# Output projections as seven half-size products, with weight sums made in DRAM

## The chip, the cores and the metric

The kernel runs on one core of a Trainium2 chip. The metric is device time in microseconds (us); lower is better. The engines are TensorE (PE: matmuls into PSUM, with PEld for the load of the stationary side), VectorE (DVE), ScalarE (ACT), GpSimd (POOL) and SyncE (SP, which issues most DMAs). Three runs of the kernel before took 1337.84, 1338.29 and 1338.46 us.

## The reference

The reference is a trunk of two layers on 512 tokens of width 2048, all in float32. Each layer is one mixer with two groups of heads, and an RMS norm closes the trunk:

```python
for l in range(DEPTH):                       # 2
    h = rmsnorm(x, attn_norm_g[l])
    qa, ka, va, ga, cq, ckv, kr, gb = jnp.split(h @ w_in[l], SPLIT_POINTS, axis=-1)
    ya = swa_attention(qa, ka, va, swa_sinks[l]) * jax.nn.silu(ga)      # 16 heads of 64, window 128
    yb = mla_attention(cq, ckv, kr, ...) * jax.nn.silu(gb)              # 8 latent heads of 128, causal
    x = x + jnp.concatenate([ya, yb], axis=-1) @ w_out[l]               # 512x2048 @ 2048x2048
return rmsnorm(x, final_norm_g)
```

The change concerns the line with `w_out`, the residual beside it and the last norm.

## The kernel before

**Products in three parts.** Every operand is split into a part `hi`, rounded by a cast on ACT, and the rest `lo`, a subtraction on DVE; `split` does both. A product is three matmuls, hi x hi, hi x lo and lo x hi (`mm3`, lines 115 to 118).

**The stream.** All dense products (input projection, gates, output projection) are one list, `stream`, of pieces. A `Piece` is four row blocks of 128 of one column tile of 128: it loads 512 KB for two pieces on SP's queue into one of three raw buffers (`RBUF`), splits a 128x512 part, and then gives four steps of three matmuls, 128x128 weights against 512 tokens. Weights are the stationary side; the result has features on partitions and tokens along the free axis. `prefetch` issues loads and splits `AHEAD` (3) items ahead of their use. `fill(n)` takes n steps from the stream; the attention code calls it between its own parts, with the counts in `FILLS`, so that PE has dense work while ACT and DVE do the softmax.

**Heads.** Each of eight turns does two sliding-window heads and one latent head: scores (`swa_scores`, `mla_scores`), softmax, transposes of the probabilities on PE (`swa_transpose`, `mla_transpose`; their results are split on DVE and ACT), products with the values, and the gate (`gated`, line 827), which gives `y`, a block of 128 features x 512 tokens. `put_y` keeps it, and it is split when the output projection begins.

**Output projection.** For each of 16 column tiles, 16 row blocks x 3 matmuls add up in one PSUM bank. `out_fin` (layer 0) adds the residual, which `load_res` fetched by DMA, squares the sum on ACT, adds the square into `acc` on POOL (`square_into`, line 176), stores x to DRAM and splits it for layer 1. `token_sums` (line 152) later turns `acc` into sums per token by matmuls with ones. The first layer's x is squared in the same way while it is loaded. In layer 1, `last_fin` does the adding and squaring, and the last three column tiles are computed for 256 tokens at a time, so that `finish` can scale and store the first half while the second is computed.

**What sets the order.** The program is written for a framework that orders each engine's instructions itself, by the program's order as priority and by what it reckons to be ready; tiles from a pool wait until a buffer is free. At run time each engine executes its list in order, and waits where an operand is not there.

## Time and profile before

| | |
|---|---|
| median of three runs | 1338.29 us |
| span of the profiled execution | 1336.3 us |
| PE, DVE, ACT, POOL busy | 99%, 65%, 48%, 6% |
| output projection of layer 0 | about 516 to 690 us |
| output projection of layer 1, with the end | about 1163 to 1336 us |
| DMA traffic | 131.73 MB, 99 GB/s on average |

The profiled execution's own time is known by its span; the runs' median lies 2.0 us above it. Busy times of PE overlap (a matmul starts before the one before it has drained), so work on PE is counted by the distance from one start to the next. DVE's overlap a little too. A wait names the instruction that released the waiting one.

### The profile page before, as it was taken

Reading aid. Unit: us, or ns where it says so; the run is one execution under the profiler, and the core shown is the slowest. Engines: PE = TensorE matmul, PEld = TensorE weight load, DVE = VectorE, ACT = ScalarE, POOL = GpSimd, SP = SyncE. Lnnn points to the kernel's source line nnn. Section 1 sums busy time; section 2 is a strip of 40 time slices with the busy share of each in tenths; the row PEclk is TensorE's granted clock in tenths of the full one; section 3 lists DMA queues with packets and bytes.
Section 4 is the critical chain, followed back from the end, with each engine's and each line's share of the span. In section 5 each row is a group of like instructions: output and inputs, shape, how many; then the busy total and the mean of one; then the engine's idle time right before and its main releaser. Section 6 shows DMA issues by size and latency. Waiting matters only on the chain.

```text
span 1336.3 us, 18300 instructions
## 1 busy us (share of the span) xinstructions
PE 1320.6 (99%) x6534; PEld 1114.7 (83%) x6534; DVE 867.2 (65%) x2067; ACT 637.0 (48%) x1373; POOL 78.2 (6%) x77
## 2 busy tenths in 40 slices
PE   9999999999999999999999999999999999999996
PEld 6888888888888888888888888888888888888896
DVE  5578877777777786444434787776876878733344
ACT  5546545555544564333323454554554555543331
POOL 4310000000000000111101000000000000011112
PEclk9999999999999999999999999999999999999998
DMA  6532221222221224444333313213213222233333
GB/s 205 173 122 69 80 86 59 79 89 72 79 81 64 72 68 145 147 146 149 116 88 113 120 54 107 79 49 96 80 54 105 65 65 84 88 114 126 123 103 126
DMA packets 49739, 131.73 MB, mean 99 GB/s; under 512 B 5584, under 2 KB 12800, under 8 KB 49648
## 3 DMA queue, kind: packets, MB, share of 16 engines
q1 hardware_dynamic: 49136, 129.54, 30.5%
q8 instruction: 51, 0.84, 0.3%
q0 software_dynamic: 512, 1.03, 0.2%
q14 instruction: 40, 0.33, 0.1%
HBM read 122.15 MB, written 8.39 MB: 98 GB/s over the span
## 4 chain that ended last, share of the span: by engine, by line
PE 96%; DVE 2%; ACT 1%; DMA 1%; issue 0%; SPq 0%; DVEq 0%; ACTq 0%
PE ps L116 29%; PE ps L117 29%; PE ps L118 29%; PE ps L661 2%; PE ps L806 1%; PE ps L637 1%; PE ps L597 1%; PE ps L596 1%; PE ps L781 1%; PE ps L780 1%; PE ps L287 1%; PE ps L286 1%; PE ps L152 0%; DMA blk<-in_xT 0%; PE ps L167 0%; DMA wraw<-in_w_lr 0%
## 5 line engine op out<-in xcount | busy, mean ns | idle before, releaser
L116 PE MATMUL ps<-blk,whi 128*128 128x512 f32 x1456 | 573.7, 394 | 0.3 <-ACT blk L112 0.3
L117 PE MATMUL ps<-blk,whi 128*128 128x512 f32 x1456 | 568.0, 390 | 0.3 <-DVE blk L113 0.3
L118 PE MATMUL ps<-blk,wlo 128*128 128x512 f32 x1456 | 567.7, 390 | 0.0
L108 ACT CAST whi<-wraw 128x512 fp32r<-128x512 f32 x356 | 221.0, 621 | 406.7 <-PE ps L117 380.0
L109 DVE TENSOR_TENSOR wlo<-wraw,whi 128x512 fp32r<-128x512 f32 x356 | 248.3, 699 | 187.8 <-ACT whi L108 183.3
L118 PEld LDWEIGHTS ps<-blk,wlo 128*128 128x128 f32 x1456 | 273.3, 188 | 58.1 <-DVE wlo L109 0.2
L116 PEld LDWEIGHTS ps<-blk,whi 128*128 128x128 f32 x1456 | 273.8, 188 | 54.1 <-ACT blk L112 0.7
L117 PEld LDWEIGHTS ps<-blk,whi 128*128 128x128 f32 x1456 | 273.9, 188 | 53.9 <-DVE blk L113 0.9
L176 POOL TENSOR_TENSOR blk<-blk 128x512 f32<-128x512 f32 (+1 forms) x52 | 65.9, 1268 | 1240.8 <-ACT blk L175 1240.6
L116 PE MATMUL ps<-blk 128*128 128x256 f32 (+3 forms) x376 | 123.9, 329 | 0.6 <-ACT blk L108 0.6
L117 PE MATMUL ps<-blk 128*128 128x256 f32 (+3 forms) x376 | 122.5, 326 | 0.0
L118 PE MATMUL ps<-blk 128*128 128x256 f32 (+3 forms) x376 | 122.5, 326 | 0.0
L108 ACT CAST blk<-blk 128x512 fp32r<-128x512 f32 (+2 forms) x146 | 81.5, 576 | 48.5 <-DVE blk L644 21.0
L109 DVE TENSOR_TENSOR blk<-blk 128x512 fp32r<-128x512 f32 (+2 forms) x146 | 90.9, 636 | 13.7 <-ACT blk L108 7.0
L116 PEld LDWEIGHTS ps<-blk 128*128 128x128 f32 x376 | 71.3, 190 | 8.0 <-ACT blk L108 2.2
L109 DVE TENSOR_TENSOR blk<-ps,blk 128x512 fp32r<-128x512 f32 (+2 forms) x116 | 64.9, 585 | 19.4 <-ACT blk L108 16.5
L117 PEld LDWEIGHTS ps<-blk 128*128 128x128 f32 x376 | 71.3, 190 | 6.3 <-DVE blk L109 0.4
L118 PEld LDWEIGHTS ps<-blk 128*128 128x128 f32 x376 | 71.2, 189 | 5.7 <-DVE blk L109 0.4
L616 ACT ACTIVATE blk<-blk,sm 128x256 f32<-128x256 f32 (+1 forms) x128 | 60.1, 471 | 23.9 <-DVE sm L614 22.9
L108 ACT CAST blk<-ps 128x512 fp32r<-128x512 f32 (+2 forms) x116 | 54.7, 509 | 34.2 <-PE ps L118 22.2
L113 DVE SCALAR_TENSOR_TENSOR blk<-blk,g_in_sb 128x512 fp32r<-128x512 f32 x32 | 34.1, 1066 | 26.3 <-ACT blk L112 26.2
L604 DVE CUSTOM_DVE_ANT_0 blk<-ps,dist_sb,sdiv_sb 128x256 f32<-128x256 f32 x96 | 43.3, 479 | 0.8 <-PE ps L597 0.8
(156 smaller groups left out, 1137.9 us busy)
## 6 DMA issues: line engine op xcount, KB each, us to landing
wraw<-in_w_in SPq DMA_DIRECT2D x104, 512.0 KB, 3.5
wraw<-in_w_out SPq DMA_DIRECT2D x58, 512.0 KB, 3.5
wraw<-in_w_lr SPq DMA_DIRECT2D x32, 352.0 KB, 3.0
blk<-in_xT SPq DMA_DIRECT2D x32, 256.0 KB, 3.7
blk<-in_w_kv SPq DMA_DIRECT2D x16, 256.0 KB, 4.2
x_scr<-blk SPq DMA_DIRECT2D x16, 256.0 KB, 2.1
blk<-x_scr SPq DMA_DIRECT2D x16, 256.0 KB, 3.8
out_x<-blk SPq DMA_DIRECT2D x16, 256.0 KB, 2.6
```

The costliest lines, as they stand in the source:

```text
L108: nc.scalar.copy(hi, src)
L109: nc.vector.tensor_tensor(out=lo, in0=src, in1=hi.bitcast(F32), op=ALU.subtract)
L113: nc.vector.scalar_tensor_tensor(out=lo, in0=src, scalar=g, in1=hi.bitcast(F32), op0=ALU.mult, op1=ALU.subtract)
L116: nc.tensor.matmul(ps, lhsT=lh, rhs=rh, start=first, stop=False)
L117: nc.tensor.matmul(ps, lhsT=lh, rhs=rl, start=False, stop=False)
L118: nc.tensor.matmul(ps, lhsT=ll, rhs=rh, start=False, stop=last)
L176: nc.gpsimd.tensor_tensor(out=acc, in0=acc, in1=sq, op=ALU.add)
L286: nc.tensor.matmul(ps[5], lhsT=hb[:, P:2 * P], rhs=ah, start=kt == 0, stop=False)
L287: nc.tensor.matmul(ps[5], lhsT=hb[:, P:2 * P], rhs=al, start=False, stop=kt == KT - 1)
L604: nc.vector.tensor_tensor_reduce(out=pt, in0=o, in1=bias, scale=1.0, scalar=sdiv_sb[:, l, h:h + 1], op0=ALU.add, op1=ALU.max, accum_out=mx ...
L616: nc.scalar.activation(pv[qb], pv[qb], AF.Exp, bias=nb[:, qb:qb + 1], scale=SLOPES[h], accum_out=sm[:, qb:qb + 1])
L661: nc.tensor.matmul(av[:, w], lhsT=st.VS[kb // 2][:, (kb % 2) * 2 + g, :], rhs=t_[:, w], start=n == 0, stop=n == len(jobs) - 1, skip_group_ ...
```

## The change

The output projection is computed by a scheme of seven products of half size (Strassen's, in Winograd's form), once for each of two column groups g. Its two-by-two blocks are the first and second 256 tokens, the even and odd blocks of y, and the column tiles g and g + 2 of 512. Four sums of weight blocks are made in DRAM (`t_scr`) by plain and accumulating DMAs on POOL's queue, listed by `plan_sums` and issued by `tprep` every fifth step. The left factors are sums and differences of y's blocks and token halves, made on DVE (`put_y`, `build`). Tokens are now the stationary side: a result has 128 tokens on partitions and 512 features along the free axis. The seven products add up in three pairs of banks (X, Z, Y); `prod_fin` joins them, and `emit` adds the residual by an accumulating DMA into the block that the product left. Squares are summed per token by ACT itself. `Trans` turns layer 0's result back to features on partitions by transposes on PE. The last norm is done for each token tile (`finish`).

```diff
+SAHEAD = 6
+LAG = 10
+TSTEPS = 5
+BLOCKS = {1: (0, 0), 2: (1, 0), 3: (1, 1)}
+SUMS = {5: 0, 6: 1, 7: 2, 4: 3}
+STAGE = {1: "A", 7: "A", 5: "B", 6: "B", 2: "D", 4: "D", 3: "C"}
+ACCUM = {1: "X", 2: "X", 5: "Z", 3: "Z", 6: "Y", 7: "Y", 4: "Y"}
...
-    x_scr = dram.tile([KT, P, S], F32, name="x_scr")
+    x_scr = dram.tile([S, D], F32, name="x_scr")
+    t_scr = [dram.tile([4, 2, 4, P, 1024], F32, name=f"t_scr{l}") for l in range(L)]
...
+            need(self.st, STAGE[self.q], self.k)
+            o = (self.k % 2) * 512
+            if self.mate is not None:
+                raw = self.mate.raw
+            else:
+                raw = wp.tile([P, 1024], F32, tag="wraw", name="wraw", bufs=RBUF)
+                if self.pair:
+                    nc.sync.dma_start(raw, self.src())
+                    self.raw = raw
+                else:
+                    nc.sync.dma_start(raw[:, o:o + 512], self.src()[:, o:o + 512])
+            if self.keep or self.k % 2:
+                hi, lo = blk(F32R), blk(F32R)
+            else:
+                hi = wp.tile([P, 512], F32R, tag="whi", name="whi")
+                lo = wp.tile([P, 512], F32R, tag="wlo", name="wlo")
+            split(raw[:, o:o + 512], hi, lo)
+            self.hl = (hi, lo)
...
+            nc.tensor.matmul(ps, lhsT=sh[:, t], rhs=hi, start=new, stop=False, **kw)
+            nc.tensor.matmul(ps, lhsT=sh[:, t], rhs=lo, start=False, stop=False, **kw)
+            nc.tensor.matmul(ps, lhsT=sl[:, t], rhs=hi, start=False, stop=self.last, **kw)
+            if self.last:
+                prod_fin(st, self.g, self.q, s)
...
+            for t in range(NB):
+                nc.tensor.transpose(ps[:, t * P:(t + 1) * P], st.xt[t, kt // 4][:, c:c + P], identity=ident)
+            hi, lo = blk(F32R), blk(F32R)
+            split_scaled(ps, g_in_sb[:, st.l, kt:kt + 1], hi, lo)
+            st.acts[kt] = (hi, lo)
...
+        t, b = t_scr[l], w_out[l]
+        for g in range(2):
+            for kk in range(4):
+                cp(t[0, g, kk], b[0, 0, g, kk])
+                cp(t[2, g, kk], b[0, 1, g, kk])
+                add(t[0, g, kk], b[0, 1, g, kk])
+                add(t[2, g, kk], b[1, 1, g, kk])
+                cp(t[1, g, kk], t[0, g, kk])
+                add(t[1, g, kk], b[1, 1, g, kk])
+                cp(t[3, g, kk], t[1, g, kk])
+                add(t[3, g, kk], b[1, 0, g, kk])
...
+            run_late()
+            if pos["n"] % TSTEPS == 0 and not isinstance(it, Prod):
+                tprep(1)
...
+            if stage == "A" and y0 is not None:
+                hi, lo = blk(F32R), blk(F32R)
+                split(y0, hi, lo)
+                st.S[1, k] = (hi[:, :H], lo[:, :H])
+                st.S[7, k] = (hi[:, H:], lo[:, H:])
+            elif stage == "B" and y0 is not None and y1 is not None:
+                s = blk()
+                nc.vector.scalar_tensor_tensor(out=s[:, H:], in0=y0[:, H:], scalar=-1.0, in1=y1[:, H:],
+                                               op0=ALU.mult, op1=ALU.subtract)
+                nc.vector.tensor_tensor(out=s[:, :H], in0=s[:, H:], in1=y0[:, :H], op=ALU.add)
+                hi, lo = blk(F32R), blk(F32R)
+                split(s, hi, lo)
+                st.s12[k] = s
+                st.S[5, k] = (hi[:, :H], lo[:, :H])
+                st.S[6, k] = (hi[:, H:], lo[:, H:])
...
+        if j % 2 == 0:
+            nc.vector.tensor_tensor(out=y[:, H:], in0=y[:, :H], in1=y[:, H:], op=ALU.subtract)
...
+        if q == 1:
+            st.a[s] = blk()
+            nc.scalar.copy(st.a[s], ps)
+        elif q == 6:
+            st.u[s] = blk()
+            nc.vector.tensor_tensor(out=st.u[s], in0=ps, in1=st.a[s], op=ALU.add)
+            if g == 1 and st.l == L - 1:
+                xv = st.xv.pop(s)
+                nc.vector.tensor_tensor(out=st.u[s], in0=st.u[s], in1=xv, op=ALU.subtract)
+        elif q == 7:
+            w = blk()
+            nc.vector.tensor_tensor(out=w, in0=ps, in1=st.a[s], op=ALU.add)
+            nc.vector.tensor_tensor(out=w, in0=st.acc_ps["Z", s], in1=w, op=ALU.subtract)
+            emit(st, 2 + s, 2 + g, w)
+        elif q == 2:
+            c = blk()
+            nc.scalar.copy(c, ps)
+            emit(st, s, g, c)
+        elif q == 4:
+            a = st.a.pop(s)
+            nc.vector.tensor_tensor(out=a, in0=ps, in1=a, op=ALU.add)
+            emit(st, 2 + s, g, a)
+        elif q == 3:
+            u = st.u.pop(s)
+            nc.vector.tensor_tensor(out=u, in0=ps, in1=u, op=ALU.subtract)
+            emit(st, s, 2 + g, u)
...
+        if not last:
+            nc.gpsimd.dma_start(c, xsrc(st, t, f), accum_op=ALU.add)
+            sq = blk()
+            nc.scalar.activation(sq, c, AF.Square, accum_out=st.ss[:, t * 4 + f:t * 4 + f + 1])
...
+            if f == 3 and t < 2:
+                nc.vector.scalar_tensor_tensor(out=c, in0=c, scalar=r, in1=st.gf[f], op0=ALU.mult, op1=ALU.mult)
+            elif i % 2:
+                nc.scalar.activation(c, c, AF.Copy, scale=r)
...
+            if g == 0:
+                r += seq(g, 1, range(7)) + seq(g, 5, range(7)) + seq(g, 1, [7]) + seq(g, 6, range(7))
+                r += seq(g, 5, [7]) + seq(g, 6, [7])
+            else:
+                r += seq(g, 1, range(8)) + seq(g, 5, range(8)) + seq(g, 6, range(8))
+                if st.l < L - 1:
+                    r += [Trans(layers[st.l + 1], kt) for kt in range(4)]
+            r += seq(g, 2, range(4)) + seq(g, 7, range(8)) + seq(g, 2, range(4, 8)) + seq(g, 4, range(8))
...
-    wo = w_out.reshape(L, 2, 8, P, D).transpose(0, 2, 1, 3, 4).reshape(L, D, D)
+    wo = w_out.reshape(L, 2, 4, 2, P, 2, 2, 512).transpose(0, 1, 5, 6, 2, 4, 3, 7).reshape(L, 2, 2, 2, 4, P, 1024)
```

What the change removes: `load_res`, `out_fin`, `last_fin`, the old `finish` with its spread by matmuls, and the squares that POOL added up after the first layer's input.

How the order of the instructions moves, in three places. In the first, POOL's queue stands at the start of the program; L176 (now L181) adds the squares of layer 0's x, one row block after the other, and the names DMASW are semaphores of POOL's own DMAs. Before:

```order
L70 DMA qsc_sb<-in_qscale 128x8 [waits DMASW0_49]
L70 DMA isl_sb<-in_islope 128x16 [waits DMASW1_49]
L70 DMA sink_sb<-in_sinks 128x32 [waits DMASW2_49]
L176 TENSOR_TENSOR blk<-blk 128x512 [waits Activation_49]
L176 TENSOR_TENSOR blk<-blk 128x512 [waits Activation_49,Pool_49] x14
```

Now, from the third of these adds on (`t_scr_117` holds layer 0's weight sums):

```order
L181 TENSOR_TENSOR blk<-blk 128x512 [waits Activation_49,Pool_49]
L386 DMA t_scr_117<-in_w_out 512x256 [waits DMASW4_49,DMASW2_49]
L181 TENSOR_TENSOR blk<-blk 128x512 [waits Activation_49,Pool_49]
L386 DMA t_scr_117<-in_w_out 512x256 [waits DMASW5_49,DMASW3_49]
L383 DMA t_scr_117<-t_scr_117 16x8192 [waits DMASW6_49,DMASW4_49]
L181 TENSOR_TENSOR blk<-blk 128x512 [waits Activation_49,Pool_49]
L383 DMA t_scr_117<-in_w_out 16x8192 [waits DMASW7_49]
L386 DMA t_scr_117<-in_w_out 512x256 [waits DMASW6_49,DMASW0_49]
L383 DMA t_scr_117<-in_w_out 16x8192 [waits DMASW1_49]
L181 TENSOR_TENSOR blk<-blk 128x512 [waits Activation_49,Pool_49]
L383 DMA t_scr_117<-t_scr_117 16x8192 [waits DMASW0_49]
L386 DMA t_scr_117<-in_w_out 512x256 [waits DMASW7_49]
```

The adds, which followed each other, now have the sums' copies (L383) and accumulating DMAs (L386) between them, each waiting for the DMA whose result it needs.

The second place is VectorE in layer 0's last turn of heads, around the latent head's scaled probabilities (L795, now L978) and the own-block products of the sliding-window transposes (L639, now L822). Before:

```order
L639 TENSOR_TENSOR blk<-ps,tri_sb 128x512
L109 TENSOR_TENSOR wlo<-wraw,whi 128x512
L793 RECIPROCAL sm<-sm 128x4
L795 TENSOR_SCALAR blk<-blk,sm 128x128
L795 TENSOR_SCALAR blk<-blk,sm 128x256
L795 TENSOR_SCALAR blk<-blk,sm 128x384
L795 TENSOR_SCALAR blk<-blk,sm 128x512
L109 TENSOR_TENSOR blk<-blk 128x512
L644 TENSOR_TENSOR blk<-ps,blk 128x256
L109 TENSOR_TENSOR wlo<-wraw,whi 128x512
L109 TENSOR_TENSOR blk<-blk 128x256
```

Now, from the last of the scaled probabilities on (L499 and L501 make the sums of y for one pair of blocks, L514 another, L114 splits):

```order
L978 TENSOR_SCALAR blk<-blk,sm 128x512
L114 TENSOR_TENSOR blk<-blk 128x512
L499 SCALAR_TENSOR_TENSOR blk<-blk 128x256
L514 TENSOR_TENSOR blk<-blk 128x256
L501 TENSOR_TENSOR blk<-blk 128x256
L114 TENSOR_TENSOR wlo<-wraw,whi 128x512
L114 TENSOR_TENSOR blk<-blk 128x512
L114 TENSOR_TENSOR blk<-wraw,blk 128x512
L822 TENSOR_TENSOR blk<-ps,tri_sb 128x512
L514 TENSOR_TENSOR blk<-blk 128x256
L114 TENSOR_TENSOR blk<-blk 128x512
L827 TENSOR_TENSOR blk<-ps,blk 128x256
```

L822 stood ahead of the scaled probabilities and now stands behind them, behind seven more instructions that make left factors and split weights.

The third place is POOL where layer 0's output projection begins to give results. Before, squares are added there:

```order
L176 TENSOR_TENSOR blk<-blk 128x512 [waits PE_49,Activation_49]
L176 TENSOR_TENSOR blk<-blk 128x512 [waits Activation_49,Pool_49] x14
L176 TENSOR_TENSOR blk<-blk 128x512 [waits DMAHW4_49,PE_49,Activation_49]
L176 TENSOR_TENSOR blk<-blk 128x512 [waits Activation_49,Pool_49]
L176 TENSOR_TENSOR blk<-blk 128x512 [waits DMAHW0_49,DMAHW2_49,PE_49,Activation_49]
```

Now (`t_scr_118` holds layer 1's weight sums; L569 adds the residual):

```order
L386 DMA t_scr_118<-in_w_out 512x256 [waits DMASW6_49,DMASW3_49]
L386 DMA t_scr_118<-in_w_out 512x256 [waits DMASW5_49]
L383 DMA t_scr_118<-t_scr_118 16x8192 [waits DMASW7_49]
L386 DMA t_scr_118<-in_w_out 512x256 [waits DMASW0_49]
L569 DMA blk<-in_x 128x512 [waits PE_49,DVE_49,Activation_49,Pool_49]
L569 DMA blk<-in_x 128x512 [waits DVE_49,PE_49]
```

The last of all 128 sums, those of layer 1 among them, stand ahead of layer 0's first residual add.

## Rows read from the trace of the kernel before

**Rows 1.** The page's busy table and its chain: engine, busy us (share) xinstructions

```profile
PE 1320.6 (99%) x6534; PEld 1114.7 (83%) x6534; DVE 867.2 (65%) x2067; ACT 637.0 (48%) x1373; POOL 78.2 (6%) x77
...
PE 96%; DVE 2%; ACT 1%; DMA 1%; issue 0%; SPq 0%; DVEq 0%; ACTq 0%
```

**Rows 2.** PE's waits: waiting line and releaser, us in total, times, longest

```profile
PE ps L167 <- DVE blk L164: 2.6, 3, 2.0
```

**Rows 3.** PE's timeline in layer 0's output projection: start, length us, instruction

```profile
574.82 0.39 PE L117 MATMUL ps<-blk,whi 128*128 128x512 f32 x1
...
581.84 0.39 PE L118 MATMUL ps<-blk,wlo 128*128 128x512 f32 x1
```

**Rows 4.** Windows: length, PE, PEld, DVE, ACT, POOL busy, PEclk, DMA share, GB/s

```profile
0.00:30.00 30.00, 27.85 (x105) 20.37 (x106) 16.80 (x32) 16.70 (x31) 13.58 (x23) 1.00 0.65 213
30.00:72.00 42.00, 42.00 (x188) 34.75 (x187) 24.87 (x45) 24.11 (x45) 15.21 (x12) 1.00 0.49 161
466.00:480.00 14.00, 14.00 (x77) 12.15 (x76) 13.97 (x30) 9.07 (x18) 0.00 (x0) 1.00 0.27 94
478.00:516.00 38.00, 38.00 (x195) 32.06 (x194) 29.00 (x85) 19.19 (x49) 0.00 (x0) 1.00 0.28 95
1134.00:1171.00 37.00, 37.00 (x191) 31.24 (x190) 28.10 (x83) 19.19 (x49) 0.00 (x0) 1.00 0.29 93
520.00:690.00 170.00, 170.00 (x752) 140.76 (x751) 71.98 (x105) 58.31 (x98) 19.48 (x15) 1.00 0.43 139
```

**Rows 5.** PE's timeline in layer 1's half-width column tiles

```profile
1317.84 0.28 PE L116 MATMUL ps<-blk 128*128 128x256 f32 x1
...
1318.08 0.28 PE L118 MATMUL ps<-blk 128*128 128x256 f32 x1
```

**Rows 6.** PE's instructions by line and shape: xcount | busy us, mean ns | idle

```profile
L116 PE MATMUL ps<-blk 128*128 128x512 f32 x136 | 53.4, 393 | 0.6 <-ACT blk L108 0.6
```

**Rows 7.** PE's timeline at the latent transposes of a head

```profile
465.50 1.25 PE L806 MATMUL ps<-ident,blk 128*128 128x128 f32 x10
```

**Rows 8.** PE's timeline at the first token sums of layer 0

```profile
71.97 0.95 PE L152 MATMUL ps<-ones,blk 128*128 128x1 f32 x8
```

**Rows 9.** DVE's timeline around layer 0's last turn of heads

```profile
466.47 2.49 DVE L109 TENSOR_TENSOR blk<-blk 128x512 fp32r<-128x512 f32 x4
468.88 0.68 DVE L109 TENSOR_TENSOR wlo<-wraw,whi 128x512 fp32r<-128x512 f32 x1
...
478.57 0.28 DVE L602 TENSOR_TENSOR blk<-ps,dist_sb 128x128 f32<-128x128 f32 x1
...
497.87 0.42 DVE L109 TENSOR_TENSOR blk<-blk 128x256 fp32r<-128x256 f32 x1
498.20 0.68 DVE L639 TENSOR_TENSOR blk<-ps,tri_sb 128x512 f32<-128x512 f32 x1
...
515.64 0.69 DVE L827 TENSOR_TENSOR blk<-ps,blk 128x512 f32<-128x512 f32 x1 [1.21 <-PE ps L118]
```

**Rows 10.** POOL's timeline: the third add of squares

```profile
17.31 1.29 POOL L176 TENSOR_TENSOR blk<-blk 128x512 f32<-128x512 f32 x1 [0.80 <-ACT blk L175]
```

**Rows 11.** DMA issues by line: queue, xcount, KB each, median us to landing

```profile
wraw<-in_w_in SPq DMA_DIRECT2D x104, 512.0 KB, 3.5
...
sin_sb<-in_sin POOLq DMA_DIRECT2D x1, 256.0 KB, 6.1
...
qsc_sb<-in_qscale POOLq DMA_DIRECT2D x1, 4.0 KB, 5.8
...
sink_sb<-in_sinks POOLq DMA_DIRECT2D x1, 16.0 KB, 4.4
```

**Rows 12.** The timeline at the end, from the stream's last matmul on

```profile
1322.04 0.28 PE L118 MATMUL ps<-blk 128*128 128x256 f32 x1
...
1324.15 0.16 DVE L182 TENSOR_SCALAR sm<-ps 128x2 f32<-128x2 f32 x1 [1.37 <-PE ps L152]
...
1328.21 4.33 SPq L430 DMA_DIRECT2D out_x<-blk  x8
```

More of the change, by code (lines that the diff above doesn't have):

```diff
@@ L283, in step @@
                 s = slice(i * P, (i + 1) * P)
[L284 to L290 removed]
+                mm3(ps[i], hi[:, s], lo[:, s], ah, al, self.first, self.last)
@@ new lines, in trunk_kernel, with __init__, load, ready @@
+    class Trans:
+        n = 1
+        ahead = AHEAD
+        def __init__(self, st, kt):
+            self.st, self.kt = st, kt
+        def load(self):
+            pass
+        def ready(self):
+            return all((t, self.kt // 4) in self.st.xt for t in range(NB))
+        def step(self, j):
+            st, kt = self.st, self.kt
+            c = (kt % 4) * P
+            ps = bank()
+            for t in range(NB):
[3 more added lines that the diff above has]
+            st.acts[kt] = (hi, lo)
@@ L413, in finish @@
[L413 to L430 removed]
+        build(st)
@@ L433, in trunk_kernel, with link @@
+    def link(items):
+        for a, b in zip(items, items[1:]):
+            if (a.g, a.q) == (b.g, b.q) and a.k % 2 == 0 and b.k == a.k + 1:
+                a.pair, b.mate = True, a
     marks = {}
@@ L435, in trunk_kernel @@
         st = layers[l]
-        stream += [Low(l, kt, st.low) for kt in range(KT)]
+        kts = list(range(KT)) if l == 0 else [*range(4), *range(8, 12), *range(4, 8), *range(12, 16)]
+        for n, kt in enumerate(kts):
+            if l > 0 and n >= 4 and n % 1 == 0 and n < 12:
+                stream.append(Trans(st, kts[n + 4]))
+            stream.append(Low(l, kt, st.low, n == 0, n == KT - 1))
         marks[l, "low"] = len(stream)
+        plan_sums(l)
         st.kv = {}
```

312 lines of the change are left out of this document (172 added, 140 removed).

## The prediction

> **What bounds the kernel now.** I read the page's busy table first, then PE's waits, then single engines where the change lands. PE is busy 99% of the span, and the chain that ended last is 96% PE [rows 1]. The line for which PE waited longest in total cost it 2.6 us in 3 waits [rows 2]. So the time is the sum of PE's matmuls plus a start and a tail. In the output projection the matmuls follow each other at (581.84 - 574.82) / 31 = 0.2265 us [rows 3], whatever their busy time of 0.39 us says, since they overlap. VectorE (DVE) is the next engine, 65% on the page, but not evenly so: in 466 to 480 us it is busy 13.97 of 14 us, and during the last head 29.00 of 38 and 28.10 of 37 us, against 72 of 170 us in the first projection [rows 4]. The profiled span is 1336.3 us; the runs' median of 1338.29 lies 2.0 us above it. I sum against the span and add 2.0.
>
> **PE: what goes.** Layer 0's projection is 16 tiles x 16 rows x 3 = 768 matmuls of 512 columns. The new one is 7 products x 2 column groups x 8 row blocks x 2 token blocks x 3 = 672. That is 96 x 0.2265 = 21.8 us less. Layer 1 had 13 x 48 = 624 of these and 288 of 256 columns, which follow each other at (1318.08 - 1317.84) / 2 = 0.12 us [rows 5]: 141.3 + 34.6 = 175.9 us, against 672 x 0.2265 = 152.2, so 23.7 us less. That tokens are now the stationary side should not matter: attention's 128x512 matmuls, with other operands, have a mean of 393 ns, as the stream's 0.39 us [rows 3, 6]. New are 64 transposes that bring the token-major residual back: ten take 1.25 us with the last one's 0.28 in it, so 0.108 each and 7.0 us in all [rows 7]. The token sums before layer 1 and inside the last stage and one spread leave the stream; eight sums take 0.95 us [rows 8], so about 1.6 us. Net on PE: -21.8 - 23.7 + 7.0 - 1.6 = -40.1 us.
>
> **VectorE in the last head of each layer.** This is the term against the change. Every product needs its own weight split, 112 per layer instead of 64, since a split now serves 6 matmuls instead of 12; and the seven left factors are built from y on DVE. The listing of DVE's order shows where they fall: before the splits that the last head's transposes wait for. DVE's work from the last head's first score to its gate stands in the order as before plus 9 splits of y or its sums, 10 weight splits and 22 operations of 128x256. Splits follow each other at (468.88 - 466.47) / 4 = 0.60 us, a 128x256 one takes (498.20 - 497.87) = 0.33 [rows 9]. So 19 x 0.60 + 22 x 0.33 = 18.7 us are added to a stretch that takes 515.64 - 478.57 = 37.1 us in layer 0 [rows 9] (in layer 1 it is 1134 to 1171 us), and in which DVE is idle about 9 us [rows 4]. PE's work in it stays as it was. If DVE never idles, the stretch grows by 18.7 - 9 = 9.7 us; if all of its idle time stays (it waits there for ScalarE's exponentials and for PE's scores), by 18.7. DVE's order is fixed, so what stands behind a late build is the split of the transposed probabilities; PE stands at the attention products behind that, and the stream's own matmuls behind PE. I take 12 per layer, near the lower end, because the builds are ready early and fill the idle time: +24 us, bounds 19 to 37. Behind the gate DVE has less than PE again: 92 splits and some 40 other operations are about 78 us beside 540 x 0.2265 = 122 us of matmuls. ScalarE is not the limit: 19.19 of 38 us now [rows 4], and 19 casts more at 0.545 make 30 of 47.
>
> **The sums on POOL's queue.** The weight sums are 128 DMAs of 512 KB from DRAM to DRAM, half of them accumulating, and the order puts them on POOL from the first microseconds on, not where the program's text has them: 28 stand between the fifteen adds of squares whose total the first token sums on PE wait for, and all 128 stand ahead of layer 0's first residual add. Each dependent one waits on POOL for the one before it. On the first stretch nine such waits follow each other (six for an accumulating DMA, three for a copy) from the add at 17.31 + 1.3 us on [rows 10]; PE asks for the total at 71.97 [rows 8]. With L the mean time from issue to completion, POOL is through at about 20.5 + 9 L, so L up to 5.7 us costs nothing. Over the whole queue eight DMAs make three links, 32 x 3 = 96 L from 18.6 us on; the first residual add is wanted at about 477 + 49 (216 product matmuls) + 12 (the head's own) + 12 = 550 us, and loads split six items ahead cover some 7 more: L up to (557 - 18.6) / 96 = 5.6 us. No row shows a copy within DRAM or an accumulating DMA. Lower bound: a 512 KB load by SP lands in 3.5 us; upper: twice the 6.1 us that 256 KB took on POOL's queue at the start, 12 us [rows 11]. The nearest rows are that queue's own: even 4 and 16 KB took 5.8 and 4.4 us there. I take 5.5 for a copy and 6.5 for an accumulation at the start, 5.0 and 6.0 later: 20.5 + 39 + 16.5 = 76 us, 4 late, and 2 more for the low-rank squares, which stand behind two further links: +6 us. Later 32 x (6.0 + 10.0) = 512 us from 18.6 on ends at 531, in time.
> The Trainium skill, "DMA: Bandwidth & Descriptors", section "Anatomy of one DMA", prices a DMA of this queue at 2.0 us plus bytes / 436 GB/s, an estimate of 3.2 us here; the 3.5 us of SP's load is close to it, the 5.8 us of 4 KB is not. By it the +6 would be 0 and the time 1322.
>
> **The product stage's other waits.** A load of 512 KB now serves 12 matmuls, 2.72 us, so 193 GB/s, plus 8.4 MB of residual reads and stores in 155 us, 54 GB/s. The start moved 213 GB/s at a busy share of 0.65 [rows 4], that is 328 at full share; 247 is 0.75 of it. Three raw buffers give a load 8.2 us for landing (3.5) and two splits (1.2). The residual is added by a DMA into the block that the product left; ScalarE squares it ten steps, 6.8 us, later, and 256 KB on POOL's queue took 6.1 [rows 11]. What would queue behind a late square are the casts of the next weights, which run six items (8.2 us) ahead. I take +2 us, bounds 0 to 10.
>
> **Tail.** Now 1336.3 - 1322.3 = 14.0 us from the last matmul to the end; the root's chain on small tiles begins at 1324.15, and the last stores start at 1328.21 [rows 12]. The new tail needs no matmul and no spread, but DVE's order has three token tiles' chains behind the last product: subtract and square 1.3, three times 2.4 (six or seven small operations at 0.2, a root, two scalings), issue and landing 3.1: about 12. -2 us, bounds -5 and 0.
>
> **Sum.** 1336.3 - 40.1 + 24 + 6 + 2 - 2 = 1326.2, and with 2.0 around the span 1328 us.
>
> **Rivals.**
> *POOL's chain decides (slower side).* L is above 5.7 us. At the start PE then waits 9 L - 51.5 us at the token sums, and SP's load of w_kv, which waits for a buffer that POOL's squares release, holds up every weight load behind it; at the first residual add, 96 L - 538 us. At L = 5.8 it is about 1 + 19 instead of the 6 that I have: 1342; at 6.0, 3 + 38: 1363; at 6.2, 4 + 57: 1383. It makes the kernel slower from L = 5.8 on. For it: POOL's queue needed 4.4 to 6.1 us for 4 to 256 KB [rows 11], an accumulation reads twice, and by 72 us the loads (213 x 30 + 161 x 42 = 13.2 MB) and the sums' 14 MB, 21 with what accumulation reads, would need (13.2 + 21) / 0.328 = 104 us. Against: the start's DMAs were queued behind each other, and in the last heads the DMA engines are busy 0.28 of the time [rows 4].
> The Trainium skill, the same page, "Issuing engines are not separate DMA queues", says that DMAs of all issuers run on the same 16 engines and interleave; the trace of before, where POOL's queue moved only 1 MB, neither shows nor denies it.
> *VectorE keeps up.* The builds fall into its idle time and PE loses under 8 us in both heads together: 1336.3 - 40.1 - 2 + 2 + 6 + 2.0 = 1304. For it: before, DVE was saturated for 14 us just ahead of the last head and PE did not wait [rows 4]; that work is now spread. Against: 18.7 us do not fit into 9.
> *Loads bound the products.* If landing rises from 3.5 to 9 us, a pair takes (9 + 1.5) / 3 = 3.5 us instead of 2.72, and 112 pairs cost 87 us: above 1400. It decides from about 6.7 us on. Against: landing stayed near 3.5 us at 0.65 share.
>
> **How the numbers follow.** Forecast 46% (its own range 1318 to 1340), POOL's chain 28%, VectorE keeps up 18%, loads 8%. Predicted: 1328. Range 1304 to 1362: below lies half of the second rival, above the worse half of the first and the third. A measurement of this kernel can tell 0.2% (2.7 us) from no change. Faster: 40 of the forecast's 46 and the 18 = 58%; same: 4 of the forecast, 4 of POOL's = 8%; slower 34%.
>
> **What would show it.** PE's waits: at the first token sums of layer 0, up to 10 us on POOL (none: L below 5.7; 20 or more: first rival). In the last head of each layer 9 to 15 us on DVE's splits, none elsewhere in attention. In the products gaps under 1 us; gaps on casts that wait for a DMA speak for the third rival, a long wait of the square on ScalarE near 557 us for the first. Matmul spacing of 0.2265 also in the products. The sums' DMAs from issue to landing: 5 to 6.5 us. I am wrong at the root if PE's busy sum does not fall by about 40 us.

## The result and the profile after

The changed kernel takes 1408.8 us (median of four runs, 1405.2 to 1413.4), the kernel before 1338.4 in the same session: a ratio of 1.053, 95% interval [1.051, 1.055]. Forecast were 1328, range 1304 to 1362. The profiled execution is the one of 1405.2 us; its span is 1403.4 us, 67.1 more than before.

Four lines of the changed kernel's page; the first answers to that of [rows 1]. (The page's chain breaks off after 4% of the span and shows nothing here.) Each digit stands for a slice of 35.1 us:

```profile
PE 1321.9 (94%) x6234; PEld 1089.0 (78%) x6234; DVE 965.8 (69%) x2278; ACT 698.7 (50%) x1535; POOL 158.4 (11%) x195
...
PE   8859999999999996999989999999999999789894
...
PEclk9989999999999997999999999999999999889998
DMA  8999999999942222586762422222312312257766
```

There are 300 matmuls fewer, yet PE's busy sum is what it was (1320.6), and it stands for 81 us (1403.4 - 1321.9), where it stood for 16. PE's digits are lowest in the third slice (70 to 105 us), in the sixteenth (526 to 561 us), from 1193 to 1263 us and at the end, and PEclk, the granted clock, falls in the same places. PE's longest waits, which answer to the single line of [rows 2] (releaser, us in total, times, longest), name no main culprit:

```profile
PE ps L157 <- POOL blk L181: 13.3, 1, 13.3
PE ps L334 <- ACT blk L113: 12.2, 7, 3.7
PE ps L334 <- ACT whi L113: 7.0, 2, 3.7
PE ps L121 <- ACT blk L117: 6.8, 6, 2.6
PE ps L121 <- DVE blk L555: 3.7, 1, 3.7
```

So I cut both spans at instructions that both kernels have (first scores, rotary scores, last gates, first latent products), at their starts in the two timelines, and set each stretch beside the forecast's term for it:

| stretch, us | before | after | change | forecast |
|---|---|---|---|---|
| start to layer 0's first score | 129.1 | 160.9 | +31.8 | +6 |
| seven heads, either layer | 353.4 | 353.3 | -0.1 | 0 |
| layer 0's last head: last rotary score to last gate | 33.1 | 55.6 | +22.5 | +12 |
| from there to layer 1's first latent product | 151.5 | 152.1 | +0.6 | -17 (-21.8 + 3.5 + 1) |
| layer 1's latents to its first score | 117.5 | 120.4 | +2.9 | +2 |
| layer 1's last head | 33.1 | 55.0 | +21.9 | +12 |
| from there to the end | 165.2 | 152.8 | -12.4 | -25 (-23.7 + 1 - 2) |

Nearly everything lies in three kinds of place: the start, the last heads and the two stages behind the last gates, which I call layer 0's and layer 1's product stage. Between them the kernels run alike. The same stretches as windows of the changed kernel (length, PE, PEld, DVE, ACT, POOL busy, PEclk, DMA share, GB/s), to be read against [rows 4]:

```profile
0.00:30.00 30.00, 25.80 (x92) 17.33 (x92) 14.72 (x28) 13.55 (x27) 14.88 (x25) 1.00 0.83 244
30.00:72.00 42.00, 35.58 (x139) 26.58 (x139) 18.37 (x34) 17.43 (x35) 16.08 (x18) 0.96 1.05 284
...
514.00:570.00 56.00, 44.47 (x168) 32.19 (x167) 44.01 (x104) 29.06 (x67) 0.00 (x0) 0.82 0.30 91
570.00:722.00 152.00, 141.58 (x608) 114.94 (x608) 85.50 (x143) 75.76 (x151) 14.09 (x16) 0.96 0.73 210
722.00:1195.00 473.00, 472.40 (x2369) 400.07 (x2368) 338.76 (x864) 236.43 (x534) 4.21 (x3) 1.00 0.27 82
```

At 30 to 72 us the DMA engines are full by their share (1.05, before 0.49) and PE's matmuls fall from 188 to 139. In the last head it is not DMA (0.30): PE stands for 11.5 of 56 us, and the granted clock is 0.82 on average.

### The profile page after: what moved, and what is told of

It is laid out like the page before. It is cut to its first block, busy times and chain, and to the rows that moved or that the text cites. A ratio compares the mean times of both kernels' runs of the same rounds, so it can differ in the third digit from the quotient of the medians.

```text
span 1403.4 us, 18287 instructions
## 1 busy us (share of the span) xinstructions
PE 1321.9 (94%) x6234; PEld 1089.0 (78%) x6234; DVE 965.8 (69%) x2278; ACT 698.7 (50%) x1535; POOL 158.4 (11%) x195
## 5 line engine op out<-in xcount | busy, mean ns | idle before, releaser
L121 PE MATMUL ps<-blk,whi 128*128 128x512 f32 x992 | 395.8, 399 | 11.2 <-ACT blk L117 6.8
L122 PE MATMUL ps<-blk,whi 128*128 128x512 f32 x992 | 390.2, 393 | 2.8 <-DVE blk L118 2.5
L123 PE MATMUL ps<-blk,wlo 128*128 128x512 f32 x992 | 388.7, 392 | 0.0
L114 DVE TENSOR_TENSOR wlo<-wraw,whi 128x512 fp32r<-128x512 f32 x348 | 243.2, 702 | 115.2 <-ACT whi L113 109.4
L121 PEld LDWEIGHTS ps<-blk,whi 128*128 128x128 f32 x992 | 187.9, 189 | 50.5 <-ACT blk L117 10.1
L122 PEld LDWEIGHTS ps<-blk,whi 128*128 128x128 f32 x992 | 188.0, 190 | 41.5 <-DVE blk L118 7.1
L123 PEld LDWEIGHTS ps<-blk,wlo 128*128 128x128 f32 x992 | 187.3, 189 | 40.5 <-DVE wlo L114 0.4
L114 DVE TENSOR_TENSOR blk<-blk 128x512 fp32r<-128x512 f32 (+2 forms) x178 | 109.5, 621 | 22.9 <-ACT blk L113 16.1
L114 DVE TENSOR_TENSOR blk<-wraw,blk 128x512 fp32r<-128x512 f32 x116 | 78.4, 687 | 36.5 <-ACT blk L113 36.0
L334 PE MATMUL ps<-whi,blk 128*128 128x512 f32 x216 | 89.6, 415 | 13.5 <-ACT whi L113 7.0
L334 PE MATMUL ps<-blk 128*128 128x512 f32 x232 | 94.1, 413 | 8.8 <-ACT blk L113 8.7
L121 PE MATMUL ps<-blk 128*128 128x512 f32 (+2 forms) x280 | 96.5, 345 | 0.6 <-ACT blk L113 0.6
L335 PE MATMUL ps<-blk 128*128 128x512 f32 x232 | 94.7, 408 | 1.1 <-DVE blk L114 0.9
L122 PE MATMUL ps<-blk 128*128 128x512 f32 (+2 forms) x280 | 95.3, 340 | 0.0
L123 PE MATMUL ps<-blk 128*128 128x512 f32 (+2 forms) x280 | 95.3, 340 | 0.0
L336 PE MATMUL ps<-blk 128*128 128x512 f32 x232 | 93.0, 402 | 0.0
L335 PE MATMUL ps<-wlo,blk 128*128 128x512 f32 x216 | 88.1, 408 | 0.0
L336 PE MATMUL ps<-whi,blk 128*128 128x512 f32 x216 | 87.3, 408 | 0.1
L113 ACT CAST blk<-wraw 128x512 fp32r<-128x512 f32 x116 | 70.4, 616 | 30.0 <-DMA wraw<-t_scr 15.0
L114 DVE TENSOR_TENSOR blk<-ps,blk 128x512 fp32r<-128x512 f32 (+2 forms) x116 | 65.0, 585 | 28.5 <-ACT blk L113 25.2
```

The lines of the kernel that those rows point to most:

```text
L113: nc.scalar.copy(hi, src)
L114: nc.vector.tensor_tensor(out=lo, in0=src, in1=hi.bitcast(F32), op=ALU.subtract)
L121: nc.tensor.matmul(ps, lhsT=lh, rhs=rh, start=first, stop=False)
L122: nc.tensor.matmul(ps, lhsT=lh, rhs=rl, start=False, stop=False)
L123: nc.tensor.matmul(ps, lhsT=ll, rhs=rh, start=False, stop=last)
L334: nc.tensor.matmul(ps, lhsT=sh[:, t], rhs=hi, start=new, stop=False, **kw)
```

## The experiments

Every kernel starts from the changed one unless it says otherwise; times are medians, and the kernel before stood at 1338.3 to 1338.8 throughout. A, B and C are the theories of the expectation quoted above each result. Stages are read from one profiled execution of each kernel.

**1. The start.** e2_late_sums: each group of copies first waits for a tiny DMA from a tile that comes late.

```
+ nc.gpsimd.dma_start(t_scr[l][i, g, kk][0:1, 0:4], src[0:1, 0:4])   # src: st.R, then y of heads 0 to 6
```

> All weight sums are still made, by the same copies and accumulating DMAs, but each group of eight waits for a tiny DMA from a tile that exists only later: the first two groups for the row of norm factors of layer 0 (about 100 us), the other fourteen two by two for the gated outputs of heads 0 to 6. Theory A (what costs at the start is that the sums run beside the input loads and in front of GpSimd's adds): the first attention score of layer 0 comes at 129 us again, as before the change, not at 160.9; nothing else moves; 1409 - 32 = 1377 us. Rival B (76 MB of extra traffic cost what they cost wherever they run): the heads, in which TensorE is full now, get gaps of 10 to 30 us in all, and the time stays at 1390 to 1409. Rival C (sums so late that the products wait for them): casts of TensorE's weights wait on loads from the scratch tensor for more than 7 us in a last head, time over 1380.

e5_join:

```
- nc.gpsimd.tensor_tensor(out=acc, in0=acc, in1=sq, op=ALU.add)
+ nc.vector.tensor_tensor(out=acc, in0=acc, in1=sq, op=ALU.add)
```

> Only the 21 additions of squares move from GpSimd to VectorE; the sums stay where they are, at the start. Theory A (the start is late mostly because the sums' transfers compete with the input loads): only GpSimd's 13.3 us wait before the first token sums goes; the latent products still end near 85 us (before the change 69), the first score comes at 146 to 150 us, time about 1396. Rival B (the start is late because GpSimd's queue is taken by DMA issues, which hold its additions back, and squares and splits behind them): the latent products end near 70 us, the first score comes at 129 to 133, time about 1378.

e2 took 1389.8 us, e5 1405.3. In e2 the first score came at 129.6 us, so A holds for the start. But layer 0's last head took 69.6 us, with casts waiting 25.1 us for loads of sums, as C said: the second layer's sums ran beside it. In e5 PE's wait on POOL was gone and nothing was won: the latent products ended at 101.7 us, the score came at 162.1. Both theories had the wrong number; what falls is that POOL's adds alone made the start late. PE now waited for the input's splits, and the casts in them (L117; L112 in the kernel before) for their loads. These waits between 30 and 110 us, before, in the changed kernel and in e5:

```profile
ACT blk L112 <- DMA blk<-in_xT: 3.5, 9, 0.8
```

```profile
ACT blk L117 <- DMA blk<-in_xT: 27.0, 10, 5.3
```

```profile
ACT blk L117 <- DMA blk<-in_xT: 40.6, 12, 7.2
```

e5 moved more than it says. Freed of the adds, POOL had issued 23 sums by 72 us, where the changed kernel had issued 17, so the loads met more of them. It shows that the sums make the start as late without POOL's adds; it does not show that PE's 13.3 us behind POOL cost the changed kernel nothing. The issues of the changed kernel, of e5 and of e2 (queue, xcount, KB, median us to landing):

```profile
t_scr<-in_w_out POOLq DMA_DIRECT2D x96, 512.0 KB, 9.1
...
t_scr<-t_scr POOLq DMA_DIRECT2D x32, 512.0 KB, 6.7
blk<-in_xT SPq DMA_DIRECT2D x16, 256.0 KB, 6.2
```

```profile
blk<-in_xT SPq DMA_DIRECT2D x16, 256.0 KB, 8.1
```

```profile
blk<-in_xT SPq DMA_DIRECT2D x16, 256.0 KB, 3.2
```

The input's loads go by SP's queue, the sums by POOL's; beside the sums the loads land in 6.2 and 8.1 us, without them in 3.2. The DMA share counts the time that packets took, so no run tells whether the 16 engines or the DRAM behind them was short. c1_late starts each layer's sums in one go, layer 0's at its norm factors, layer 1's at that layer's first gated output:

```
+ if l == 0: start_sums(l, st.R)              # all 8 groups, each behind its tiny DMA
+ if l == 1 and i == 0: start_sums(l, y)
```

> All weight sums are made, each layer's in one run: layer 0's wait for its row of norm factors (about 100 us), layer 1's for the first gated output of layer 1 (about 840 us). The run that paced them over heads 0 to 6 of layer 0 gave the start back (first score at 129.6 us) but its last head in layer 0 grew from 55.6 to 69.6 us, with casts waiting 25.1 us for loads of sums. Theory A (that came of the second layer's sums running beside the last head's weight loads): the first score stays at 129 to 130, the last head of layer 0 is 55 to 56 us again, time 1374 to 1379. Rival B (the sums' traffic costs the same wherever it runs): time 1387 to 1409.

1370.8 us, 3 under A's range: first score at 129.5, the last head 54.6. The same 128 DMAs of 512 KB cost 38 us in one place (34 between the profiled executions) and next to nothing in another: the seven heads beside them take 353.3 us, as ever.

**2. The last heads.** e3_no_left_sums (leaves work out, see its expectation):

```
- s = blk(); (two VectorE operations from y0, y1)
+ s = y1
- nc.vector.tensor_tensor(out=s[:, H:], in0=s[:, H:], in1=y1[:, :H], op=ALU.add)
```

> Left out: the three sums of gated outputs per pair of blocks (24 VectorE instructions of 128x256 per layer); the products 5, 6 and 3 take the odd gated output itself in their place, with as many splits as before. The last head of each layer is 55.6 us from its first rotary score to the last gate, before the change 33.1 (515.6 - 482.5). Theory A (VectorE's sums, made just before they are used, stand in the chain sum, cast, difference, matmul): 24 x 0.335 us = 8 us less VectorE work and the cast's wait on them (8.6 us) gone, and less time at the lower clock: the last head falls by 10 to 16 us in each layer, time 1377 to 1389. Rival B (the 19 further splits alone fill VectorE and ScalarE): it falls by less than 5 us a layer, time over 1399.

1379.4 us, the last heads 42.5 and 42.4: A. In the changed kernel one such item reads (timeline of all engines; brackets: idle before, releaser):

```profile
543.95 0.42 DVE L499 SCALAR_TENSOR_TENSOR blk<-blk 128x256 f32<-128x256 f32 x1
...
544.62 0.42 DVE L501 TENSOR_TENSOR blk<-blk 128x256 f32<-128x256 f32 x1
...
545.08 0.62 ACT L113 CAST blk<-blk 128x512 fp32r<-128x512 f32 x1 [1.85 <-DVE blk L501]
...
545.73 0.69 DVE L114 TENSOR_TENSOR blk<-blk 128x512 fp32r<-128x512 f32 x1 [0.68 <-ACT blk L113]
...
546.27 0.79 PE L334 MATMUL ps<-blk 128*128 128x512 f32 x1 [0.48 <-ACT blk L113]
```

Sum, cast, difference go back and forth between DVE and ScalarE, each waiting for the other: ScalarE 1.85 us for the sum, DVE 0.68 us for the cast. So DVE is neither full nor free: 44.01 of 56 us busy, and late.

Two changes that move the sums won nothing. c3_pool (with c1_late's sums and e4_lag's lag, below) makes them on GpSimd, whose negation took 1.28 us and each sum 0.73:

```
+ nc.gpsimd.tensor_scalar(... scalar1=-1.0 ...); nc.gpsimd.tensor_tensor(... subtract); nc.gpsimd.tensor_tensor(... add)
```

> Three changes together: the weight sums late as in c1_late, the squares 24 steps behind as in e4_lag, and the left-factor sums on GpSimd (negate, subtract, add of 128x256, and the later add, 32 per layer; half of the 1.548 us that its 128x512 addition took is 0.77 us each) in place of VectorE's 24 of 0.335 us. Theory A (VectorE was the full engine of the last head; the parts add up): 1409 - 32 - 15 - 2 x 8 to 13 = 1336 to 1346 us, last heads of 42 to 48 us. Rival B (the sum's own latency counts, and GpSimd's 2.3 us in place of 0.84 us is late for the cast): the last heads stay at 53 us or more, time over 1356.

1367.1 us, last heads 57.1 and 58.9: B. (With the same lag and late sums, but the sums of y on VectorE, it is 1363.1, 54.5 and 55.9: f1_late_lag below.) ScalarE's casts waited 10.4 us for POOL in layer 0's. With the low parts of products 1 and 7 on GpSimd too (c7_pool_a) it was 1371.8 and 61.0, by its rival B.

d1_order lets the last heads work on products 1 and 2, which need no sums:

```
- seq(g, 1, range(7)) + seq(g, 5, range(7)) + seq(g, 1, [7]) + seq(g, 6, range(7)) ...
+ seq(g, 1, range(7)) + seq(g, 2, range(7)) + seq(g, 1, [7]) + seq(g, 5, range(7)) + seq(g, 2, [7]) ...
```

> One change of the changed kernel: the last heads work on the products 1 and 2, whose left factors are single gated outputs (only splits), in place of 1 and 5; product 2 gets its own bank, and the left-factor sums are made later, in the product stages, where VectorE is busy 55 to 65%. Everything is computed. Theory A (the sums late on a full VectorE made the last heads long, as e3_no_left_sums showed by leaving them out: 42.5 us in place of 55.6): the last heads are 42 to 46 us, the product stages as before, time 1380 to 1390. Rival B (the sums cost the same where they go: casts of the product stage then wait for them): the last heads shrink but the product stage of layer 0 grows from 152 to 160 us or more, time over 1396.

1431.0 us, last heads 57.7 and 57.2, and by neither theory. Its longest waits of PE:

```profile
PE ps L989 <- DVE blk L852: 23.7, 2, 12.0
PE ps L334 <- DVE blk L536: 17.7, 4, 6.3
PE ps L334 <- DVE blk L852: 11.3, 2, 5.6
```

Product 5 still came up before the last gate, its sums and splits now in one row, and the attention's own addition (L852), which PE needs, stood behind them in DVE's order: PE waited 11.6 us there. And product 7, now right behind 6 in the same bank, waits until DVE has read it (L536). With late sums and lag this order gave 1388.0 (d2_all; 1330 to 1356 were expected), with items prepared 9 ahead in place of 6 it was 1397.1 (d3_ahead; expected 8 to 20 us under d2 or within 4 of it), the last heads 61.6 and 62.1 us where d2 has 57.9 and 57.6. I read it so, without a run that isolates it: more work ahead, on a queue that runs in order, is more work in front of what is urgent.

f4_no_split, from c6_floor (below), gives every product the parts of a key tile:

```
- split(y0, hi, lo)        # and the other three splits of left factors
+ hi, lo = st.KH[0], st.KL[0]
```

> As c6_floor, and also left out: the casts and differences of all left factors (32 casts and 32 differences per layer); the products take the parts of a key tile in their place. Theory A (what is left in the last heads of c6_floor, 44 us against 33.1 before the change, is these splits on ScalarE and VectorE): the last heads are 32 to 35 us, time 1310 to 1318. Rival B (it is the chain of weight loads and casts for products of two token tiles): 39 us or more, time over 1325.

Last heads 34.8 and 35.9, against c6_floor's 44.1 and 43.9: A, to within 1 us. The time, 1323.7 us, is over A's and just under B's: the heads gave 17 us, but the stages behind them took 148.1 and 149.4 us (145.1 and 147.3). So leaving out the sums takes 13 of a last head's 22 us, leaving out the splits 9.

**3. The clock.** f3_dummy puts matmuls of a zero factor in front of the items for which PE waits:

```
+ if self.q == 5 and self.g == 0 and self.k < 7 and j == 0:
+     for _ in range(12):
+         nc.tensor.matmul(st.acc_ps["X", 0][:, :H], lhsT=zero_r, rhs=st.S[1, 0][0], start=False, stop=False, ...)
```

> The changed kernel with 84 further 128x256 matmuls per layer, of a zero left factor, added into an open sum (which they leave as it is): 12 ahead of each of product 5's first seven items in the last head, where TensorE waits most. At 0.113 us each they are 9.5 us of work per layer; TensorE waits about 11.5 us in a last head, over half of it at these items. Theory A (the granted clock falls to the lower level because TensorE stands still in these waits): the clock in the last head, 0.50 to 0.85 in the slices with waits, is at 1.00 or near it at these items, the other matmuls there lose no time to it (7.7 us per last head), and the last head is 48 to 55 us, in spite of 9.5 us more work: time 1394 to 1408. Rival B (the clock falls for another reason): it stays low, the last head is 58 us or more, time over 1412.

1401.3 us. The same stretch in the changed kernel, then in f3 (third value from the right: granted clock):

```profile
526.00:530.00 4.00, 1.44 (x8) 0.98 (x7) 3.53 (x15) 1.70 (x7) 0.00 (x0) 1.00 0.00 0
530.00:534.00 4.00, 2.33 (x5) 1.66 (x6) 3.50 (x10) 2.06 (x5) 0.00 (x0) 0.52 0.07 17
534.00:538.00 4.00, 3.89 (x11) 2.25 (x9) 3.88 (x9) 1.88 (x4) 0.00 (x0) 0.63 0.20 62
...
546.00:550.00 4.00, 3.35 (x12) 2.30 (x12) 3.31 (x8) 1.35 (x3) 0.00 (x0) 0.85 0.41 133
```

```profile
526.00:530.00 4.00, 4.00 (x31) 3.74 (x30) 3.73 (x16) 1.50 (x7) 0.00 (x0) 1.00 0.00 0
530.00:534.00 4.00, 4.00 (x30) 3.74 (x29) 3.30 (x10) 2.07 (x7) 0.00 (x0) 1.00 0.04 9
534.00:538.00 4.00, 4.00 (x28) 3.52 (x27) 3.99 (x9) 2.16 (x4) 0.00 (x0) 1.00 0.23 71
...
546.00:550.00 4.00, 3.22 (x12) 2.02 (x12) 3.32 (x8) 1.35 (x3) 0.00 (x0) 1.00 0.34 133
```

With PE kept at work the clock is 1.00; past the last of these items it falls again (0.50 at 554 to 562 in f3). A holds for the clock: it falls behind the waits. What this costs is less than A had it. The last head took 54.8 us, not 55.6, and from 18 us into it on the matmuls that both kernels have start within 1.2 us of each other. Their busy time in it fell from 44.1 to an estimated 38.9 us (48.4 less the 9.5 added), yet the next items came no sooner. This suggests that most of what the low clock took there was time in which PE would have waited anyway. PE's timeline in the changed kernel shows the lower clock:

```profile
531.67 1.22 PE L334 MATMUL ps<-blk 128*128 128x512 f32 x2 [3.65 <-ACT blk L113]
...
534.09 0.63 PE L336 MATMUL ps<-blk 128*128 128x512 f32 x1
534.51 0.63 PE L334 MATMUL ps<-whi,blk 128*128 128x512 f32 x1
```

After 3.65 us of standing, matmuls follow each other at 0.42 us, not at the 0.2265 of [rows 3]: 1.2 in place of 2.4 GHz. Over the whole run the same 6234 matmuls are busy 1321.9 us here and 1291.4 in f2_no_resid, the least disturbed version below; by the mean granted clocks, 0.970 and 0.989, an estimated 42 and 15 us of clock were lost. So most of the 30 us is clock. How much of it the kernel's time pays, no run shows.

**4. The product stages.** e4_lag:

```
- later(rest)            # LAG = 10
+ later(rest, lag)       # 24; 16 or 10 for the last blocks of a layer
```

> The square that follows a residual-adding DMA is placed 24 product steps behind the DMA's issue, no longer 10 (16 or 10 where the end of a layer needs it). Theory A (in the product stages ScalarE stands at squares for DMAs that take 6.3 to 7.0 us, 32.4 us in layer 0 and 22.5 us in layer 1, its casts come late, and TensorE loses the gap and runs at the lower clock after it): those waits nearly go, the stage from the last gate to the first latent product of layer 1 falls from 152.1 us by 8 to 15, layer 1's by 3 to 8, time 1386 to 1398. Rival B (the casts wait for weight loads anyway, or the clock is low for another reason): the same gaps stand with another releaser, time within 4 us of 1409.

1393.8 us, within A; layer 0's product stage is 145.5 us, 6.6 less where A had 8 to 15, layer 1's to the end 146.7, 6.1 less. f1_late_lag joins it to c1_late:

> The late weight sums of c1_late and the squares 24 steps behind as in e4_lag, nothing else; everything is computed. The left-factor sums stay on VectorE, since GpSimd (c3_pool, 1367.1 us with both of these) and the other order (d2_all, 1388.0) made it no better. Theory A (the two costs are separate): 1409 - 38 - 15 = 1356 us, last heads 53 to 56 us, the product stage of layer 0 145 to 146 us. Rival B (with the weight sums late the loads that held up the squares are gone, so the lag gives nothing more): 1366 to 1371.

1363.1 us, between the two: layer 0's stage 145.1, layer 1's 147.9. c6_floor leaves out both kinds of sums and keeps the lag:

> Left out: the weight sums (the products 4 to 7 load a single block of weights in place of a sum, the same bytes) and the left-factor sums (as in e3_no_left_sums); the squares are 24 steps behind. So the three costs found are away together, and the products, their splits and loads are left. Theory A (the costs are separate): 1409 - 32 - 2 x 13 - 15 = 1336 us; what lies between that and the 1296 to 1300 us of the pure TensorE sum is the splits in the last heads (42 us each against 33 before the change) and the gaps of the product stages. Rival B (each shortage lengthened the others, and the lower clock after a gap fed on them): 1310 to 1328 us, mean granted clock 0.99.

1337.1 us, as A. With sums of both kinds left out and the lag the change is worth nothing (ratio 0.999 [0.998, 1.000]). f2_no_resid takes the residual out of that as well:

```
- nc.gpsimd.dma_start(c, xsrc(st, t, f), accum_op=ALU.add)
```

> As c6_floor, and also left out: the 30 DMAs that add the residual. In c6_floor the product stage of layer 0 still took 145.1 us; 151.5 before, less 21.8 for fewer products, plus 3.5 for transposes, makes 133. Theory A (the waves of residual-adding DMAs share the 16 engines with the weight loads, the share is 1.07 at 560 to 570 us, casts wait 50.7 us for loads there, and TensorE then waits 3.5 us and runs at the lower clock): the stage falls by 4 to 8 us, layer 1's by 2 to 6, time 1323 to 1332. Rival B (three load buffers and their casts set the pace, not the other transfers): time 1334 to 1338.

1322.7 us, layer 0's stage 134.0 and layer 1's 142.2: A, and more than it expected (11.1 and 5.0 us). Is it the bytes or the form? g1_plain, from f1_late_lag:

```
- nc.gpsimd.dma_start(c, xsrc(st, t, f), accum_op=ALU.add)
+ xr = blk(); nc.sync.dma_start(xr, xsrc(st, t, f))
+ nc.vector.tensor_tensor(out=c, in0=c, in1=xr, op=ALU.add)   # in rest(), ahead of the square
```

> As f1_late_lag, with the residual loaded by plain DMAs of SyncE's queue into a tile of its own (same bytes) and added by VectorE (30 additions of 0.6 us) ahead of the square, in place of the 30 accumulating DMAs of GpSimd's queue. Theory A (the accumulating form is what costs: without these DMAs c6_floor's stages fell by 11.1 and 5.0 us): the product stage of layer 0 falls from 145.1 to 134 to 140, time 1346 to 1357. Rival B (their bytes beside the weight loads are what costs): the stage stays at 143 to 148, time 1360 to 1368.

1345.1 us, A and a little more: the same bytes by another way cost less. Layer 0's stage in f1_late_lag, then in g1_plain:

```profile
537.80:682.90 145.10, 137.94 (x608) 112.66 (x607) 85.77 (x143) 74.90 (x151) 14.15 (x16) 0.98 0.74 220
```

```profile
536.60:670.60 134.00, 134.00 (x609) 111.26 (x608) 95.34 (x159) 77.10 (x154) 0.00 (x0) 1.00 0.74 243
```

The same DMA share, more bytes per second, and PE never stands. What SP's queue waits for in that stage suggests a reason, in f1 and in g1:

```profile
SPq L308 <- DVE blk L114: 54.9, 26, 10.9
SPq L582 <- DMA blk<-in_x: 33.6, 13, 5.5
```

```profile
SPq L308 <- DVE blk L114: 65.6, 28, 12.1
...
SPq L585 <- DVE blk L581: 6.0, 4, 2.8
```

L308 loads weights; its wait for a free raw buffer is as long in g1, where PE never stands. L582 and L585 store a finished block to the scratch for layer 1. In f1 the store cannot start before the accumulating DMA has landed, and the weight loads of the next products stand behind it on SP. A plain load can be issued before the product is there to be added to, and the store then waits for DVE alone. g1 changes queue and moment with the form; which of them counts was not separated, and no run moved the store alone.

g2_early makes three of the eight left sums in their own heads:

```
+ if j % 2 and j < 6: left_sum(st, j // 2)
```

> As f1_late_lag, with the left-factor sums of the first three pairs made in their own heads (0 to 2), where VectorE has room; no more tiles are free for the other pairs. Theory A (the sums, made just before use, lengthen the last heads by 13 us each, in proportion to their number): 3 of 8 pairs give 3 to 6 us per last head, time 1351 to 1357. Rival B (the tiles that they hold delay something else, or one late pair is enough to hold up the row): 1361 or more.

1354.2 us, last heads 50.0 and 50.9 against f1's 54.5 and 55.9: A. This is not free: the seven heads, in the first of which the early sums run, take 355.2 us a layer, not 353.3. g3_both has both repairs:

> Both of g1_plain and g2_early; everything is computed. Theory A (costs are separate): 1338 to 1352 us, at or above the kernel before; Rival B: 1356 or more.

1338.8 us, 1.000 [0.999, 1.001] of the kernel before. That is the best complete version here: it wins back 70 us and reaches the old time, not less. Its product stages, 134.0 and 142.5 us, hold the whole gain of the scheme; the last heads, 49.9 and 49.7 us against 33.1, take most of it back.

## Why the prediction was wrong

*PE's term, -40.1 us, was right.* With the other costs away the stages show it: f2's are 134.0 and 142.2 against 151.5 and 165.2, -40.5 us in all, where PE's term has -42.0 for these two (-21.8 + 3.5 - 23.7). In g3, with everything computed, it is -40.2. The check that I had named for it, PE's busy sum, was a bad one: it holds clock as well as work. All else began with what PE waited for.

*"The sums on POOL's queue" failed, by 26 us of the 77.* I priced the sums as a chain of waits on POOL, asked from which L on POOL would be late, and put their traffic beside the loads of the start at nothing. That is the step that failed. POOL was late, by 13.3 us, but with its adds off POOL the start was as late (e5); with the sums moved away from the input's loads it was on time (e2, c1). My working had (13.2 + 21) / 0.328 = 104 us for loads and sums together, and used it as an argument for a rival. The token sums came at 101.5, but the agreement is partly luck: the windows show 244 to 284 GB/s at the start, not 328, and the profile's bytes on POOL's queue (76.00 MB for all sums, residuals and constants) count an accumulating DMA once, where I counted it twice.

The Trainium skill, "DMA: Bandwidth & Descriptors", section "Issuing engines are not separate DMA queues", says that the DMAs of all issuers run on the same 16 engines and interleave. A DMA share of 1.05 and input loads that land in 6.2 us, 3.2 with the sums late, agree. By the same page's "Anatomy of one DMA" a sum's DMA would be an estimated 3.2 us. Measured were 6.7 and 9.1, at a full share; my 5.0 to 6.5 were too low as well.

The first rival had half of its mechanism: the late start, not the late residual. Its other half rested on a miscount. 128 DMAs make 16 eights, not 32, and the trace has 81 waits of POOL for its own sums' DMAs, five for each eight, not 96 links. The last sum was issued at 390.7 us, where I had the end at 531, and the first residual add at 596.3. L decided nothing there.

*"VectorE in the last head" was the right mechanism at half its size, 44 instead of 24 us.* I set DVE's added work (18.7 us) against its idle time and took 12. Measured are 22.5 and 21.9, beyond the 18.7 that I had called the worst case for a head. "The builds are ready early" is the step that failed: they are prepared six items ahead, but sum, cast and difference run one behind the other, each engine idle while the other works, and PE stood waiting for them. No term had the clock either. An estimate of what it took of PE's busy time in a last head is 8 us, 44.47 x (1 - 0.82), but f3 gives no sign that it is a further part of the 22: with the clock at 1.00 for most of the head, the head was 0.8 us shorter.

*"The product stage's other waits", +2, was some 28 for the two stages*, from the changed kernel's 152.1 and 152.8 us to g1's 134.0 and 142.8. I looked at ScalarE's squares behind a landing of 6.1 us (it was 6.3 and 7.0) and found the casts covered by six items. The squares alone cost 6 us a stage (e4). What I did not follow was SP's queue: the block's store waits for the same DMA, and weight loads stand behind it. Without accumulating DMAs the stages are 11 and 5 us shorter (f1 to g1); that the store is the reason is read from SP's waits, not tested. The third rival, loads that land late, had the right symptom, casts waiting for loads, and the wrong cause: between 570 and 690 us the loads landed in 4.3 and 5.0 us, and the rival needs 6.7. They were issued late.

*The tail* was 17.5 us from the last matmul's end on, where I took 12: +3.5 us, not -2. The timeline at the end:

```profile
1384.89 0.63 ACT L573 ACTIVATE blk<-blk 128x512 f32<-128x512 f32 x1 [2.74 <-DMA blk<-x_scr]
...
1385.53 0.39 PE L336 MATMUL ps<-blk 128*128 128x512 f32 x1
...
1385.64 1.28 ACT L193 ACT_TABLE_LOAD   x1
...
1388.69 11.01 SPq L604 DMA_DIRECT2D out_x<-blk  x16
```

A square stood for a residual until 1384.89 us, the root's table load came behind it, and 16 stores take SP from 1388.69 on, where [rows 12] have 8 in 4.33 us. No run took it apart.

## What to carry to other kernels

Price a stream of background DMAs first by bytes over the stretch that it runs in, beside what that stretch must load anyway, and put it where the kernel loads little (here beside the seven heads). When PE is 99% busy, ask of each new step what stands in line behind it on every in-order queue, the store's queue too: a store of a block that a DMA has just added to waits for that landing, and so does what is queued behind the store. Do not take PE's busy sum for its work. Behind waits it held some 30 us of lower clock here, and whether that costs time depends on whether the next item is ready: in the last heads, by f3, it mostly was not.

## What the runs showed that I had not expected

- Matmuls that add nothing can be free: 168 of them in the last heads made the run no longer (1401.3 against 1408.8 us; the profiled executions, 1403.9 and 1403.4, differ by less than 1 us). They ran where PE waited, and the granted clock stayed at 1.00 beside them.
- GpSimd took 1.28 us for a 128x256 multiplication by a constant and 0.73 for a sum of two tiles of that size.
- The changed kernel's start is 32 us late whatever the latent products do: they end at 84.9, 95.8 or 101.7 us in three versions, and the first score comes between 160.9 and 162.6. The first two of these versions have the same start, so the end of the latent products differs by 11 us from one execution to another.
